# GpSimd's instructions of a decoder step issued in written order, with some mixer, feed-forward and tail steps in another order or on another engine

## The chip, the cores and the metric

The kernel runs on one core of one Trainium2 chip. The metric is the device time of one execution in microseconds (us): three runs of the kernel before took 1024.37, 1024.83 and 1026.25 us, so the median is 1024.83. The core's engines are TensorE (PE in the profile; PEld is its weight load), VectorE (DVE), ScalarE (ACT), GpSimd (POOL) and SyncE (SP), which here only issues transfers.

## The reference

One layer of a hybrid decoder is computed for 512 new prompt tokens behind 16 learned meta tokens, and for 8 running sequences of 4 new tokens each: 560 rows of 1024 in all. Cut to what matters:

```python
x = x + 0.5 * swiglu(rmsnorm(x, g_ff1), ...)          # FF1, 2816 hidden
u = rmsnorm(x, g_mix); z = u @ w_in                   # q, k, v, o, gates, x, y
# 4 mLSTM heads of 128: s = (q k^T) * exp(D - m); num = s v + w_inter * C0 q
#   den = sum(s) + w_inter * (n0 . q); h = num / max(|den|, exp(-m)); state C, n, m
# RG-LRU on 512 channels: causal conv of width 4, gates r and i,
#   h_t = a_t h_(t-1) + sqrt(1 - a_t^2) * i * xc
x = x + concat(mlstm, lru) @ w_out
x = x + 0.5 * swiglu(rmsnorm(x, g_ff2), ...)          # FF2
y = rmsnorm(x, g_final)                               # and all new states
```

## The kernel before, in words

The activations X stay in on-chip memory, transposed: 8 tiles of 128 channels by 560 rows. All products run in a split form: a number is taken apart into a high half that TensorE multiplies in one pass (whi, xh, made by a CAST on ScalarE, L259) and a low rest (wlo, xl, made on VectorE, L264), and three products replace one (L296). The weights come in tiles of 128x512 on SP's queue. The two feed-forward parts use a scheme with seven products of sums of blocks in place of eight (L409; sums on VectorE in L239 and L483). The mixer's first product begins at 384.8 us of the span, behind the first feed-forward part.

The order of the work is written out by hand: FF1, MID1, FF2, MID2 are lists of step names, and PLAN is that of the mixer. A step such as tk1 is do_tk(1); it issues a few instructions on several engines. For the engines in MANUAL (line 21) the instructions stay in the order in which the steps are written; before, these are TensorE, ScalarE and VectorE. GpSimd's instructions, and SP's, are put in an order of its own by a scheduler that reckons with modelled durations. Every engine executes its queue strictly in order, so an instruction that waits holds up all behind it on its engine.

The names that the change and the prediction's steps touch:

- acc (L378) sums the squares of X for the root of the norm, on GpSimd except the last; psn (L391) is its product with ones on TensorE.
- The mixer's set-up on GpSimd (L890 to L919): identity, masks, ones. do_wrg (L923 to L931, step rg) fills one of two gate matrices of the RG-LRU: a memset of wrg, two transfers into it, a CAST to wrgh, a subtraction to wrgl. rg1 is PLAN's first step.
- do_g (L960 to L975) is the gate product pgate. It takes two weight tiles, and for each copies 40 columns from wlo into whi on GpSimd (CAST whi<-wlo, L969), before TensorE's matmuls with that tile (L972).
- For a head h: evacuations k, q, v of the products to qT, kT, vT (L953, L955); tk and tv transpose kT and vT on TensorE (pt, L1297 to L1299), the last rows by way of a copy t on GpSimd (L1294); s and m make W, the weights times the score products (L1401, VectorE); sd adds W's pieces into D (L1407 to L1411, GpSimd); qw makes qw and qn (L1418, L1420, GpSimd); n is numerator and denominator (pn, L1430 to L1454, TensorE); cp scales the state c by its decay, eight instructions (L1512, GpSimd), and adds px (L1520, VectorE).
- For a channel tile: ex evacuates px into xp (L1112 to L1119; few columns on GpSimd, the rest on VectorE); cx is the convolution (L1127, L1129); cc makes a, th and its factors (L1175 to L1181, the last a memset of eight columns of a on GpSimd); cd multiplies them (L1187), copies eight columns into th on GpSimd (L1188), scans (L1190, VectorE) and copies the ends of hs into the output tile osm (L1191, L1192, GpSimd).
- The tail: st holds the products of three heads' final states, side by side in one bank (L815 to L818); state_out copies them out on ScalarE (L821, L822), and ScalarE's queue issues o_cp and o_small (L859, L860).

## Time and profile before

| | |
|---|---|
| median of three runs | 1024.83 us |
| the profiled execution's own time | 1024.98 us |
| its span (first to last instruction) | 1023.3 us |
| mean granted clock of TensorE | 0.995 |
| TensorE busy | 1010.1 us, 99% |
| VectorE busy | 831.6 us, 81% |
| ScalarE busy | 558.3 us, 55% |
| GpSimd busy | 119.8 us, 12% |
| transferred, mean rate | 102.85 MB, 101 GB/s |

The profile is of one execution. A timeline row gives start and length, the engine, the line, the operation, output<-inputs, shapes and a count of instructions that follow each other; in brackets stands how long the engine was idle before it, and what it waited for. The view of waits adds such idle times up by the line that waited and what released it. A window gives the busy time of each engine in a stretch, the clock that was granted to TensorE (1.00 is full speed), and the transfers.

### The profile page before, as it was taken

Reading aid. Unit: us, or ns where it says so; the run is one execution under the profiler, and the core shown is the slowest. Engines: PE = TensorE matmul, PEld = TensorE weight load, DVE = VectorE, ACT = ScalarE, POOL = GpSimd, SP = SyncE. Lnnn points to the kernel's source line nnn. Section 1 sums busy time; section 2 is a strip of 40 time slices with the busy share of each in tenths; the row PEclk is TensorE's granted clock in tenths of the full one; section 3 lists DMA queues with packets and bytes.
Section 4 is the critical chain, followed back from the end, with each engine's and each line's share of the span. In section 5 each row is a group of like instructions: output and inputs, shape, how many; then the busy total and the mean of one; then the engine's idle time right before and its main releaser. Section 6 shows DMA issues by size and latency. Waiting matters only on the chain.

```text
span 1023.3 us, 20215 instructions
## 1 busy us (share of the span) xinstructions
PE 1010.1 (99%) x7786; PEld 995.2 (97%) x7786; DVE 831.6 (81%) x1462; ACT 558.3 (55%) x1071; POOL 119.8 (12%) x198
## 2 busy tenths in 40 slices
PE   9999999999999999998999999999999999999998
PEld 8999999999999999998999999999999999999997
DVE  7988788888788797879888865799888899859774
ACT  6544555565544455475756743554555665654543
POOL 0000000000000035353651202100000000000002
PEclk9999999999999999998999999999999999999999
DMA  6222223223332334234142133223323323235222
GB/s 227 95 83 88 99 94 112 85 98 109 89 104 60 102 103 146 86 95 138 54 135 97 62 104 107 73 63 103 109 89 103 104 94 114 93 102 157 78 71 96
DMA packets 60985, 102.85 MB, mean 101 GB/s; under 512 B 8512, under 2 KB 16976, under 8 KB 60888
## 3 DMA queue, kind: packets, MB, share of 16 engines
q1 hardware_dynamic: 60200, 101.23, 30.8%
q8 instruction: 61, 1.00, 0.4%
q10 hardware_dynamic: 688, 0.32, 0.1%
q14 instruction: 36, 0.29, 0.1%
HBM read 95.20 MB, written 6.33 MB: 99 GB/s over the span
## 4 chain that ended last, share of the span: by engine, by line
PE 86%; DVE 7%; issue 2%; ACT 2%; POOL 2%; DMA 1%; SPq 0%; DVEq 0%; ACTq 0%; POOLq 0%
PE pb L409 27%; PE pad L409 20%; PE pd L296 15%; PE po L296 6%; PE pg L296 3%; PE pu L296 3%; PE pv L296 2%; PE py L296 2%; PE pq L296 2%; DVE wlo L264 2%; PE pd L792 1%; POOL c L1512 1%; PE px L296 1%; PE p L296 1%; PE pk L296 1%
## 5 line engine op out<-in xcount | busy, mean ns | idle before, releaser
L259 ACT CAST whi<-raw 128x512 fp32r<-128x512 f32 (+2 forms) x289 | 172.4, 606 | 160.7 <-PE pad L409 41.6
L264 DVE TENSOR_TENSOR wlo<-raw,whi 128x512 fp32r<-128x512 f32 (+2 forms) x289 | 197.2, 699 | 68.2 <-ACT whi L259 65.4
L259 ACT CAST whi<-s 128x512 fp32r<-128x512 f32 x180 | 111.8, 622 | 106.2 <-PE pb L409 36.4
L264 DVE TENSOR_TENSOR wlo<-s,whi 128x512 fp32r<-128x512 f32 x180 | 124.3, 692 | 12.6 <-ACT whi L259 6.5
L409 PE MATMUL pad<-q21h,whi 128*128 128x280 f32 (+1 forms) x360 | 104.2, 290 | 0.9 <-DVE X L483 0.9
L409 PE MATMUL pb<-qt4l,whi 128*128 128x280 f32 (+1 forms) x360 | 104.0, 289 | 0.0
L409 PE MATMUL pad<-q21l,whi 128*128 128x280 f32 (+1 forms) x360 | 104.0, 289 | 0.0
L409 PE MATMUL pad<-q21h,wlo 128*128 128x280 f32 (+1 forms) x360 | 104.0, 289 | 0.0
L409 PE MATMUL pb<-qt4h,whi 128*128 128x280 f32 (+1 forms) x360 | 103.9, 289 | 0.0
L409 PE MATMUL pb<-qt4h,wlo 128*128 128x280 f32 (+1 forms) x360 | 103.9, 289 | 0.0
L409 PEld LDWEIGHTS pad<-q21h,whi 128*128 128x128 f32 x360 | 67.8, 188 | 1.1 <-ACT whi L259 1.1
L409 PEld LDWEIGHTS pb<-qt4h,whi 128*128 128x128 f32 x360 | 67.9, 189 | 0.0
L409 PEld LDWEIGHTS pb<-qt4h,wlo 128*128 128x128 f32 x360 | 67.8, 188 | 0.0
L409 PEld LDWEIGHTS pb<-qt4l,whi 128*128 128x128 f32 x360 | 67.8, 188 | 0.0
L409 PEld LDWEIGHTS pad<-q21l,whi 128*128 128x128 f32 x360 | 67.8, 188 | 0.0
L409 PEld LDWEIGHTS pad<-q21h,wlo 128*128 128x128 f32 x360 | 67.8, 188 | 0.0
L239 DVE TENSOR_TENSOR s<-raw 128x512 f32<-128x512 f32 x90 | 61.5, 684 | 1.8 <-DMA raw<-in_wdn 1.8
L296 PE MATMUL pd<-hh,whi 128*128 128x280 f32 (+1 forms) x294 | 61.3, 290 | 0.6 <-ACT whi L259 0.4
L296 PE MATMUL pd<-hl,whi 128*128 128x280 f32 (+1 forms) x294 | 61.4, 290 | 0.2 <-DVE hl L557 0.2
L296 PE MATMUL pd<-hh,wlo 128*128 128x280 f32 (+1 forms) x294 | 61.2, 289 | 0.0
L378 POOL TENSOR_TENSOR acc<-acc,sq 128x560 f32<-128x560 f32 (+1 forms) x6 | 9.4, 1564 | 419.8 <-ACT sq L377 419.7
L409 PE MATMUL pb<-q11h,whi 128*128 128x280 f32 (+1 forms) x180 | 52.4, 291 | 0.0
(466 smaller groups left out, 2993.9 us busy)
## 6 DMA issues: line engine op xcount, KB each, us to landing
raw<-in_wgu SPq DMA_DIRECT2D x174, 256.0 KB, 2.7
raw<-in_wdn SPq DMA_DIRECT2D x71, 256.0 KB, 2.7
raw<-in_win SPq DMA_DIRECT2D x50, 256.0 KB, 3.3
raw<-in_wout SPq DMA_DIRECT2D x16, 256.0 KB, 3.1
raw<-in_wdn SPq DMA_DIRECT2D x18, 192.0 KB, 2.3
c<-in_c0t SPq DMA_DIRECT2D x4, 512.0 KB
out_o_cs<-c SPq DMA_DIRECT2D x4, 512.0 KB, 3.0
X<-in_xT SPq DMA_DIRECT2D x7, 280.0 KB, 5.0
```

Of the source, the lines that this page charges most:

```text
L239: dve.tensor_tensor(q[k], q[x], q[y], op=op)
L259: act.copy(ready[i][0][:, :src.shape[-1]], src)
L264: dve.tensor_tensor(lo, src, hi, op=ALU.subtract)
L296: state["mm"] = pe.matmul(ps[:, hf, :n], a[:, ws], b[k][:, c0 + hf * n:c0 + hf * n + n], start=first and j == 0 and i == 0, stop=last and ...
L378: (dve if d == KD - 1 else pool).tensor_tensor(self.acc[:, c0:], self.acc[:, c0:], s[:, c0:], op=ALU.add)
L409: pe.matmul(ps, a[:, k * P:k * P + P], b, start=first and k == 0 and i == 0, stop=k == KD // 2 - 1 and i == 2, skip_group_check=not first)
L792: pe.matmul(pd[d - TAIL][:, hf, :b - a], u[:, o:o + P], v[:, C16 + a:C16 + b], start=f == c0 and m == 0, stop=f == c1 - 1 and m == 2)
L1512: pool.tensor_scalar(c0[:, b, :], c0[:, b, :], Wb[:, b, 3:4], None, op0=ALU.mult)
```

## The change

1. GpSimd joins MANUAL: its instructions are issued in the order of the steps, like those of the other three engines.
2. In PLAN the steps gf, ge, L0, tv0, ek1, eq0 and ck1 change places; the eight scalings of c become a step of their own, cw, put behind n; cc of tile 1 is split: ci1 stands where cc1 stood, and cj1, which makes th, ti and the last form of a, behind cp0.
3. Few-column instructions of ex, cc, cd and tv (memsets and copies) go from GpSimd to VectorE. Wi's sum goes there too, and in exchange a minimum on E goes to GpSimd. The copies of m into om stand later.
4. qw adds W's last piece (32x32) into qn on GpSimd, so that n needs one matmul pair less (L1453 goes).
5. In FF1 the weight step w3 stands before the root; in MID1 ib3 and if3 before qe3; in FF2 the halves ei2, hi2, hj2 replace em2, hh2, hl2, and the residual steps rd change places.
6. In the tail each head's final state has its own bank, its copies and its transfer; y's tiles are shared out otherwise between GpSimd and VectorE; o_small goes out on SP's queue.

What GpSimd issues around the gate product, before. whi<-wlo are the gate's weights, wrg the RG-LRU's gate matrix; ones, ident and the masks are set-up:

```order
L378 TENSOR_TENSOR acc<-acc,z 128x560
L969 CAST whi<-wlo 128x4x40 x2
L378 TENSOR_TENSOR acc<-acc,sq 128x560
L890 MEMSET ident 128x128
...
L925 MEMSET wrg 128x512
L901 AFFINE_SELECT smask<-smask 32x32
L909 AFFINE_SELECT seqm<-seqm 32x8 x3
L929 CAST wrgh_5108<-wrg 128x512
L930 TENSOR_TENSOR wrgl_5109<-wrg,wrgh_5108 128x512
L925 MEMSET wrg 128x512
```

And in the changed kernel (its line numbers are 18 higher here):

```order
L378 TENSOR_TENSOR acc<-acc,z 128x560
L378 TENSOR_TENSOR acc<-acc,sq 128x560
L908 MEMSET ident 128x128
...
L943 MEMSET wrg 128x512
L919 AFFINE_SELECT smask<-smask 32x32
L927 AFFINE_SELECT seqm<-seqm 32x8 x3
L947 CAST wrgh_5108<-wrg 128x512
L948 TENSOR_TENSOR wrgl_5109<-wrg,wrgh_5108 128x512
L987 CAST whi<-wlo 128x4x40 x2
L943 MEMSET wrg 128x512
```

The two casts of the gate's weights have moved from ahead of the last acc addition to behind the set-up and the first gate matrix.

On GpSimd again, head 1's D, qw and qn, before; the copies of hs are those of channel tile 1, vT and kT those of the next transposes, c_5909 is head 1's state:

```order
L1409 TENSOR_TENSOR D<-D,W 128x272
L1418 TENSOR_TENSOR qw<-qT,Wb 128x32
L1410 TENSOR_TENSOR D<-D,W 128x144
L1420 TENSOR_TENSOR qn<-qw,C 128x32
L1411 TENSOR_TENSOR D<-D,W 16x16
L1294 COPY t_6663<-vT 128x96
L1294 COPY t_6778<-kT 128x96
L1512 TENSOR_SCALAR c_5909<-c_5909,Wb 128x128
L1188 COPY th<-C 128x8
L1512 TENSOR_SCALAR c_5909<-c_5909,Wb 128x128 x3
L1191 COPY osm<-hs 128x1
L1192 COPY osm<-hs 128x8
```

And in the changed kernel:

```order
L1438 TENSOR_TENSOR D<-D,W 128x272
L1439 TENSOR_TENSOR D<-D,W 128x144
L1440 TENSOR_TENSOR D<-D,W 16x16
L1220 COPY osm<-hs 128x1
L1221 COPY osm<-hs 128x8
L1447 TENSOR_TENSOR qw<-qT,Wb 128x32
L1449 TENSOR_TENSOR qn<-qw,C 128x32
L1451 TENSOR_TENSOR qn<-qn,W 32x32
L1540 TENSOR_SCALAR c_5909<-c_5909,Wb 128x128 x8
```

qw, which stood among the sums of D, now stands behind the two copies of hs, the scan's result; the sum with W is new; the eight scalings follow together, and the copy into th is VectorE's.

The diff, cut to its core:

```diff
-MANUAL = {mybir.EngineType.PE, mybir.EngineType.Activation, mybir.EngineType.DVE}
+MANUAL = {mybir.EngineType.Pool, mybir.EngineType.PE, mybir.EngineType.Activation, mybir.EngineType.DVE}
...
-x2 f0 cv1 p0 ex2 cf0 tk1 cp0 cx2 ck1
+x2 f0 cv1 p0 ex2 cf0 tk1 ck1 cp0 cj1 cx2
 q2 L2 s1 w1 m1 sd1 eq2 hx2 hq2
-v2 ev2 cd1 hd1 a2 ta2 ca2 b2 cb2 vm1 sk1 qw1 tb2 n1 cc2 cn1 hk2 ce0
+v2 ev2 cd1 hd1 a2 ta2 ca2 b2 cb2 vm1 sk1 qw1 tb2 n1 cw1 cc2 cn1 hk2 ce0
...
-y1 tk3 cf2 to1 hd3 ey1 gy1 ck3 so0 mo1 n3 sk3 cn3 cm3
+y1 tk3 cf2 to1 hd3 ey1 gy1 ck3 so0 mo1 n3 cw3 sk3 cn3 cm3
...
         def state(i):
-            py = st[:, 129 * i:129 * i + 129]
+            py = st[i] = mm_tile("st")[:, 0, :129]
...
         def state_out(i):
-            act.copy(cp[:, i, :], st[:, 129 * i:129 * i + P])
-            act.copy(osm[:, O_NP + i:O_NP + i + 1], st[:, 129 * i + P:129 * i + P + 1])
+            act.copy(cp[:, i, :], st[i][:, :P])
+            act.copy(osm[:, O_NP + i:O_NP + i + 1], st[i][:, P:])
+            nc.scalar.dma_start(o_cp[i], cp[:, i, :])
...
     def do_ex(ct):
-        pool.memset(xp[:, 0:3], 0.0)
-        pool.tensor_copy(smp(xp, 0, 3),
+        dve.memset(xp[:, 0:3], 0.0)
+        dve.tensor_copy(smp(xp, 0, 3),
...
     def do_cd(ct):
         dve.scalar_tensor_tensor(ti, ti, -1.0, tr, op0=ALU.mult, op1=ALU.mult)
-        pool.tensor_copy(ti[:, 528:584].rearrange("p (b j) -> p b j", j=7)[:, :, 2], C[:, H0 + 8 * ct:H0 + 8 * ct + 8])
+        dve.tensor_copy(ti[:, 528:584].rearrange("p (b j) -> p b j", j=7)[:, :, 2], C[:, H0 + 8 * ct:H0 + 8 * ct + 8])
...
     def do_qw(h):
         pool.tensor_tensor(qn, qw, n0.unsqueeze(2).to_broadcast([P, NB, 4]), op=ALU.mult)
+        qs = qn.rearrange("p b j -> p (b j)")[:32]
+        pool.tensor_tensor(qs, qs, d["W"][:32, WO[5]:WO[5] + 32], op=ALU.add)
...
     def do_n(h):
-        pe.matmul(pn[:, 1, 64:96], one_m[1][:32, :], W[:32, WO[5]:WO[5] + 32], start=True, stop=False)
-        pe.matmul(pn[:, 1, 64:96], one_m[1], d["qn"].rearrange("p b j -> p (b j)"), start=False, stop=True)
+        pe.matmul(pn[:, 1, 64:96], one_m[1], d["qn"].rearrange("p b j -> p (b j)"), start=True, stop=True)
...
+    def do_cw(h):
+        c0, Wb = D[h]["c0"], D[h]["Wb"]
+        for b in range(NB):
+            pool.tensor_scalar(c0[:, b, :], c0[:, b, :], Wb[:, b, 3:4], None, op0=ALU.mult)
...
     def do_cp(h):
-        for b in range(NB):
-            pool.tensor_scalar(c0[:, b, :], c0[:, b, :], Wb[:, b, 3:4], None, op0=ALU.mult)
```

## The prediction

> **What bounds the kernel now.** I read the page first, for the engines' shares. Its first lines:

> ```profile
> span 1023.3 us, 20215 instructions
> PE 1010.1 (99%) x7786; PEld 995.2 (97%) x7786; DVE 831.6 (81%) x1462; ACT 558.3 (55%) x1071; POOL 119.8 (12%) x198
> ```

> TensorE is busy for 1010.1 of 1023.3 us. So an edit counts by three things only: matmuls taken out, stalls of TensorE removed or made, and the clock at which it runs. GpSimd with its 12% has no throughput to speak of here; it counts by when it hands a tile over. Next the waits of TensorE, the longest first:

> ```profile
> PE pt L1297 <- DVE xp L1117: 4.0, 1, 4.0
> PE pad L409 <- DVE X L483: 0.9, 1, 0.9
> PE pd L296 <- ACT whi L259: 0.4, 1, 0.4
> PE pq L296 <- DVE kT L955: 0.3, 1, 0.3
> PE pd L296 <- DVE hl L557: 0.2, 1, 0.2
> PE pu L296 <- DVE wlo L264: 0.2, 1, 0.2
> ```

> One wait of 4.0 us is most of what there is to win. The timelines of TensorE, VectorE and GpSimd around it (start, length, engine; idle time before it in brackets) say how it came about:

> ```profile
> 460.76 0.21 POOL L1525 TENSOR_TENSOR osm<-C,Wb 128x8 f32<-128x8 f32 x1 [3.07 <-DMA Wb<-rows]
> 461.18 1.38 DVE L1190 TENSOR_TENSOR_SCAN hs<-a,th 128x584 f32<-128x584 f32 x1 [4.52 <-POOL th L1188]
> 468.57 0.17 PE L1502 MATMUL py<-wm,K5s 96*128 96x8 f32 x1
> 472.74 1.09 PE L1297 MATMUL pt<-ident,kT 128*128 128x128 f32 x4 [4.00 <-DVE xp L1117]
> ```

> GpSimd, in the scheduler's order, waits 3.07 us for a transfer, and only then copies the eight columns (L1188) for which VectorE's scan has been waiting 4.52 us. VectorE stays late from there on and frees the bank of px (L1117, its last read) just before 472.74, although px and the products behind it, up to py at 468.57, were long done. Then the windows (us, busy time of PE, PEld, DVE, ACT, POOL, granted clock, DMA) and TensorE's rows behind the wait:

> ```profile
> 470.00:472.00 2.00, 0.00 (x0) 0.00 (x0) 1.96 (x5) 0.00 (x0) 0.11 (x1) 0.63 0.06 11
> 476.77 0.65 PE L296 MATMUL pq<-xh,whi 128*128 128x272 f32 x2
> 477.22 0.48 PE L296 MATMUL pq<-xl,whi 128*128 128x272 f32 x2
> 478.80 0.42 PE L296 MATMUL pq<-xl,whi 128*128 128x272 f32 x2
> 479.06 0.41 PE L296 MATMUL pq<-xh,wlo 128*128 128x272 f32 x2
> ```

> The clock falls to half inside the stall (0.63 on the mean of 470 to 472 puts the fall at 470.5) and stays there until about 477.3, 4.6 us after TensorE goes on. In that time pairs of matmuls start 0.45 us apart (476.77 to 477.22) instead of 0.26 (478.80 to 479.06), so 4.6 x (1 - 0.26/0.45) = 2.0 us more is lost: the stall's whole price is 5.9 to 6.0 us.

> **What the change removes.** Three short waits have their late producer moved ahead in VectorE's order: X (L483) before a wlo at FF1's end, kT before the zl products, one wlo before FF1's root: 0.9 + 0.3 + 0.2 = -1.4 us. In FF2 the wait for hl (0.2) gets its product in halves, and the one for a weight (0.4) an earlier release; I take -0.4 (0 to -0.6), since another product may be late behind them. The four pairs of 32-column matmuls of the denominators go:

> ```profile
> 452.29 0.38 PE L1453 MATMUL pn<-W,ones 32*128 32x32 f32 x2
> 452.60 0.41 PE L1454 MATMUL pn<-qn,ones 128*128 128x32 f32 x2
> ```

> A pair holds TensorE for 452.60 - 452.29 = 0.31 us, four of them -1.2 us. For the 4.0 us stall: the eight-column copy is VectorE's own now, so nothing of GpSimd stands ahead of the scan, and VectorE's work behind the copy is no more than before. VectorE would have about 4.5 us in hand against 4.0 lost, and ex2 follows px at once. What is late next is the evacuation itself, about 0.2 us behind the end of py. So -3.9 and -2.0 for the clock: -5.9 us (0 if VectorE is late for another reason, which the windows below speak against).

> In the tail three pairs of copies and two DMA issues on ScalarE stand behind the last state product:

> ```profile
> 1019.02 0.27 ACT L821 COPY cp<-st 128x128 f32<-128x128 f32 x1 [3.85 <-PE st L818]
> 1019.60 0.22 ACT L822 COPY osm<-st 128x1 f32<-128x1 f32 x1
> 1020.27 0.49 ACTq L860 DMA_DIRECT2D out_o_small<-osm  x1
> ```

> With a bank for each state, two pairs (0.4 of the 0.6 us from 1019.02 to the last copy's start at 1019.60) go beside products, and the second issue (0.49) goes to another queue: -0.9 us; -0.2 if the y transfers, now shared out otherwise between queues, end last.

> **What it adds: the gate product.** This is the largest term. The timeline of GpSimd and TensorE at the stage's start:

> ```profile
> 382.64 0.98 POOL L969 CAST whi<-wlo 128x160 fp32r<-128x160 f32 x2 [2.23 <-DVE wlo L264]
> 384.47 1.68 POOL L378 TENSOR_TENSOR acc<-acc,sq 128x560 f32<-128x560 f32 x1 [0.84 <-ACT sq L377]
> 388.05 0.82 POOL L891 TENSOR_SCALAR_AFFINE_SELECT ident<-ident 128x128 f32<-128x128 f32 x1
> 388.83 0.28 POOL L895 TENSOR_SCALAR_AFFINE_SELECT cmask<-cmask 128x128 f32<-128x128 f32 x1
> 391.43 0.51 POOL L925 MEMSET wrg<- 128x512 f32 x1
> 395.25 0.67 POOL L929 CAST wrgh<-wrg 128x512 fp32r<-128x512 f32 x1 [2.35 <-DMA wrg<-in_wrg]
> 396.01 1.45 POOL L930 TENSOR_TENSOR wrgl<-wrg,wrgh 128x512 fp32r<-128x512 f32 x1
> 391.98 0.63 PE L972 MATMUL pgate<-xh,whi 128*128 128x280 f32 x2
> ```

> The scheduler had put the two casts that finish the gate's weights in front, long before TensorE wants them at 391.98. In written order they stand behind the mixer's set-up and behind rg1 (memset wrg, its DMAs, wrgh, wrgl), since rg1 is the first step of the plan. GpSimd's chain from the last acc add on: set-up and memset end 5.8 us after 386.15 (391.43 + 0.51), less 0.1 for the two V memsets that leave; then 3.3 us to the data; 0.76 to wrgl's start; 1.45; the first cast 0.7 (two span 0.98). Together 11.9 us, so the first gate matmul may start 386.15 + 11.9 = 398.05 by the old clock, where it started at 391.98: a wait of 6.1 us. What comes earlier in the feed-forward part moves both ends alike. TensorE executes in order, so px and all behind it wait too, and nothing covers it. The ends: 3.7, worked out with the first rival, and 6.4 with both casts needed. The stall is longer than the one of 4.0 us that halved the clock, so I add the same 2.0 (1.0 to 3.0, by where the next change of the clock falls): **+8.1 us**.

> By the rows above the clock fell some 1.8 us after TensorE's last matmul (470.5 against 468.57 + 0.17), and a stall of 4.0 us cost 2.0 us more. [...]

> **n1, head 1's denominators.** Rows of VectorE, GpSimd and TensorE, and of GpSimd in the next head:

> ```profile
> 490.32 0.74 DVE L953 TENSOR_TENSOR vT<-pv,r 128x560 f32<-128x560 f32 x1 [1.14 <-PE pv L296]
> 490.97 0.76 DVE L1187 SCALAR_TENSOR_TENSOR th<-th 128x584 f32<-128x584 f32 x1
> 492.88 1.53 DVE L1190 TENSOR_TENSOR_SCAN hs<-a,th 128x584 f32<-128x584 f32 x1 [1.15 <-POOL th L1188]
> 487.03 0.69 POOL L1418 TENSOR_TENSOR qw<-qT,Wb 128x32 f32<-128x32 f32 x1
> 491.71 0.50 PE L1430 MATMUL pn<-qw,c 128*128 128x4 f32 x4
> 522.10 0.19 POOL L1192 COPY osm<-hs 128x8 f32<-128x8 f32 x1
> 518.52 0.25 POOL L1418 TENSOR_TENSOR qw<-qT,Wb 128x32 f32<-128x32 f32 x1
> ```

> Before, GpSimd made qw at 487.03, 4 us ahead of need. Now the two copies of hs stand ahead of qw, so n1 waits for vT, th, scan, two copies, qw: vT and th end at 491.7, the columns' copy 0.1, scan 1.53, a hand-over 0.1, two copies and qw 0.6 by the light rows (0.19 a copy, 0.25 qw): 494.1 to 494.3, against 491.71. That is +2.6; with copies and qw at their slow rows (qw 0.69) about 3.6. VectorE itself has also more to do in this stretch: before, it reached vT with 1.14 us to spare, having started at 471.72; now it starts within 0.2 us of TensorE's transposes, and cj1's products (th, ti and a, some 2 us) come into the stretch, while TensorE gains the 2.0 us of the clock. That makes vT 0 to 1.7 us late; I take 1.2. So +3.8 (2.6 to 5.3). A stall of 3.8 us lies nearest to the one of 4.0 that halved the clock; I take +1.8 (0 to 2.0). Sum **+5.6 us**.

> **Heads 2 and 3.** GpSimd now adds W's last piece into qn ahead of D, and ahead of tk3's copy t:

> ```profile
> 564.01 0.21 POOL L1411 TENSOR_TENSOR D<-D,W 16x16 f32<-16x16 f32 x1
> 564.76 0.27 PE L1299 MATMUL pt<-ident,t 128*96 128x128 f32 x1
> ```

> D starts with the last piece of W instead of the first, which I put at 0.8 us later: its end 564.22 + 0.8, then the copy, 0.2 to 0.6 like the copies above, 565.2 to 565.6 against 564.76, with TensorE 0.3 ahead for the pair taken out: +1.0 (0.4 to 1.3). In head 2 all eight scalings stand ahead of tv3's copy: +0.3 (0 to 0.8). The 22 few-column instructions that VectorE takes over, 0.1 to 0.2 us each by the osm rows, are some 3 us over 200 us; I take 0, their cover being VectorE's idle time; without it, see the third rival. The window of the fullest part:

> ```profile
> 500.00:520.00 20.00, 20.00 (x156) 19.46 (x155) 19.02 (x31) 13.85 (x34) 5.98 (x16) 1.00 0.30 80
> ```

> **Sum.** -1.4 - 0.4 - 1.2 - 5.9 - 0.9 + 8.1 + 5.6 + 0.3 + 1.0 = +5.2 us. On the profiled execution's own 1024.98 us (its span of 1023.3 and 1.7 around it) that gives 1030.2; the median of the three runs, 1024.83, is 0.15 lower, so 1030.0 us.

> **Rivals.** First, the other side: GpSimd runs the set-up at its light pace. ident took 0.82 us and cmask, of one shape and operation, 0.28. There are five like ident (smask, two selects of seqm, wrgl); at about 0.5 each, an estimate from that pair, 2.4 us go, and the gate waits 3.7 without losing the clock; n1 at its light 2.6, also at full clock. The sum is -1.4 - 0.4 - 1.2 - 5.9 - 0.9 + 3.7 + 2.6 + 0.3 = -3.2, 1021.6 us. It turns where gate and n1 together cost under 13.7 - 5.2 = 8.5 us. Against it: VectorE does the same work beside the set-up as before. [...] Chance 0.08.

> Second, n1's stall stays small: VectorE carries a lead out of the gate's stall, n1 costs 2.6 with no loss of clock: 1027.0 us. Against it: px ties VectorE to TensorE again just before. Chance 0.16.

> Third, VectorE becomes the bound in the mixer: 19.02 of 20 us are busy in the fullest window, and the 3 us of small instructions, with 1 to 2 us of waits for each other, come out at the end: +4 to +5, 1034.5 us. It decides where VectorE has under 0.5 us in 20 to spare. Chance 0.12.

> Fourth, the change does not put the casts behind rg1 in effect: TensorE's wait turns out to be on an earlier count. Then 8.1 goes: 1021.9 us. The order of the instructions speaks against it. Chance 0.03.

> **How the numbers follow.** The forecast keeps 0.61. A measurement of this kernel can tell some 0.2% from no change, 2 us: 1022.8 to 1026.9. Faster: rivals one and four, 0.11. Same: half of the second rival (0.08) and the forecast with gate and n1 both at their lower ends (0.04), 0.12. Slower: the rest, 0.77. The range leaves out the first and fourth rival below (0.11) and the worst third of the third above (0.04): 1023.5 to 1035.0.

> **What would show it.** In the changed profile: a wait of about 6 us of pgate for the cast of whi, a window at half clock behind it; none at tk1; one of 3 to 4 us at pn for qw; no L1453 pair. I am wrong if pgate starts within 2 us of psn, or if pn follows the gates' products at once.

## The result, and the profile after

The changed kernel takes 1043.72 us (median of 6 runs, 1036.73 to 1044.99), the kernel before 1025.07 us (6 runs, 1024.37 to 1026.25): the ratio is 1.0171, with a 95% interval of 1.0144 to 1.0199. The change makes the kernel 18.7 us slower, where +5.2 us was forecast. The sign was right, the size 3.6 times too small, and the time lies outside the range. Runs of one kernel lie up to 9 us apart here, the longer ones at a lower mean clock (0.985 at 1039.57 us against 0.995 at 1030.56 in qw_ahead), so each median stands with its lowest and highest run.

The profiled execution took 1044.99 us. The head of its page:

```profile
span 1043.3 us, 20212 instructions
PE 1020.1 (98%) x7778; PEld 1004.0 (96%) x7778; DVE 835.2 (80%) x1484; ACT 559.1 (54%) x1072; POOL 122.9 (12%) x183
```

TensorE is busy for 10 us more with eight matmuls fewer. That alone says that half of the loss is no wait but slower matmuls. The other half stands in the waits of TensorE:

```profile
PE pn L1461 <- POOL qw L1447: 6.2, 1, 6.2
PE pgate L990 <- POOL whi L987: 5.6, 1, 5.6
PE pt L1328 <- POOL t L1323: 2.2, 1, 2.2
PE pv L296 <- DVE xl L367: 1.1, 1, 1.1
PE pden L1469 <- ACT zh L1293: 1.0, 1, 1.0
PE pl L1238 <- DVE c L1554: 0.8, 1, 0.8
```

The stall of 4.0 us at tk1 is gone, as are the short ones for X, kT, wlo and in FF2. In their place stand three waits for GpSimd, 14.0 us together, and three short ones. All idle time of TensorE up to its own last matmul comes to 19.0 us, against 8.9 before.

The first of the three is the gate product. GpSimd's timeline there:

```profile
382.21 1.63 POOL L378 TENSOR_TENSOR acc<-acc,sq 128x560 f32<-128x560 f32 x1 [2.99 <-ACT sq L377]
393.88 0.92 POOL L947 CAST wrgh<-wrg 128x512 fp32r<-128x512 f32 x1 [2.93 <-DMA wrg<-in_wrg]
394.89 1.41 POOL L948 TENSOR_TENSOR wrgl<-wrg,wrgh 128x512 fp32r<-128x512 f32 x1
396.25 0.80 POOL L987 CAST whi<-wlo 128x160 fp32r<-128x160 f32 x2
```

The casts of the gate's weights come last of this row of work, as forecast, 14 us after the acc addition began. The second is at tv0, in GpSimd's timeline and then TensorE's:

```profile
428.82 1.61 POOL L1054 TENSOR_SCALAR E<-E 4x560 f32<-4x560 f32 x1 [6.01 <-ACT E L1052]
430.67 0.26 POOL L1323 COPY t<-vT 128x96 f32<-128x96 f32 x1
430.98 0.32 PE L1328 MATMUL pt<-ident,t 128*96 128x128 f32 x1 [2.15 <-POOL t L1323]
```

The copy t, whose vT was there since the start of the mixer, stands behind the minimum on E, which the change gave to GpSimd and which waits 6.01 us for ScalarE. The third is n1. VectorE, GpSimd and TensorE:

```profile
496.38 0.73 DVE L971 TENSOR_TENSOR vT<-pv,r 128x560 f32<-128x560 f32 x1
498.02 1.38 DVE L1219 TENSOR_TENSOR_SCAN hs<-a,th 128x584 f32<-128x584 f32 x1
499.46 0.57 POOL L1220 COPY osm<-hs 128x1 f32<-128x1 f32 x1 [3.56 <-DVE hs L1219]
499.96 1.20 POOL L1221 COPY osm<-hs 128x8 f32<-128x8 f32 x1
501.13 0.70 POOL L1447 TENSOR_TENSOR qw<-qT,Wb 128x32 f32<-128x32 f32 x1
501.88 1.01 PE L1461 MATMUL pn<-qw,c 128*128 128x4 f32 x4 [6.20 <-POOL qw L1447]
512.71 0.81 PE L296 MATMUL px<-xh,whi 128*128 128x280 f32 x2
514.26 0.67 PE L296 MATMUL px<-xh,whi 128*128 128x280 f32 x2
514.72 0.67 PE L296 MATMUL px<-xl,whi 128*128 128x280 f32 x2
```

GpSimd has nothing to do for 3.56 us, with qw's operands long there, since the copies of hs ahead of it wait for the scan. When qw has come, n1 needs 10.8 us, from 501.88 to 512.71. In the kernel before it began at 491.71, and px followed it after 5.9 us:

```profile
497.61 0.50 PE L296 MATMUL px<-xh,whi 128*128 128x280 f32 x2
```

The windows of the changed kernel (busy time of PE, PEld, DVE, ACT, POOL, then the granted clock) say why:

```profile
396.00:400.00 4.00, 3.17 (x13) 3.17 (x14) 1.34 (x2) 0.00 (x0) 1.51 (x4) 0.50 0.14 32
432.00:436.00 4.00, 4.00 (x21) 3.74 (x21) 3.57 (x9) 1.73 (x6) 1.95 (x4) 0.62 0.23 76
504.00:508.00 4.00, 4.00 (x12) 2.80 (x12) 2.17 (x5) 0.00 (x0) 4.00 (x5) 0.50 0.00 0
508.00:512.00 4.00, 4.00 (x14) 2.70 (x12) 0.00 (x0) 0.00 (x0) 1.77 (x4) 0.50 0.00 0
516.00:520.00 4.00, 4.00 (x25) 4.00 (x24) 1.75 (x3) 2.16 (x4) 0.00 (x0) 0.72 0.37 131
```

In the stall at n1 the clock fell to half, and although TensorE then shows as busy without a gap, it stayed there through all of n1 and 5.5 us of px, until about 518.2. The changes of the clock lie at 395.4 (for 6.8 us), 432.9 (3.4), 497.8 (20.5) and 589.9 (3.4): 34 us at half clock up to the last product, against 6.8 before.

### The profile page after: what moved, and what is told of

Its sections match the earlier page's. It is cut to its first block, busy times and chain, and to the rows that moved or that the text cites. A ratio compares the mean times of both kernels' runs of the same rounds, so it can differ in the third digit from the quotient of the medians.

```text
span 1043.3 us, 20212 instructions
## 1 busy us (share of the span) xinstructions
PE 1020.1 (98%) x7778; PEld 1004.0 (96%) x7778; DVE 835.2 (80%) x1484; ACT 559.1 (54%) x1072; POOL 122.9 (12%) x183
## 4 chain that ended last, share of the span: by engine, by line
PE 87%; DVE 5%; ACT 2%; POOL 2%; issue 2%; DMA 1%; SPq 0%; DVEq 0%; POOLq 0%; ACTq 0%
PE pb L409 26%; PE pad L409 20%; PE pd L296 15%; PE po L296 6%; PE pu L296 4%; PE pg L296 4%; PE px L296 3%; PE pk L296 2%; PE pq L296 1%; PE py L296 1%; DVE wlo L264 1%; PE pn L1465 1%; PE pd L808 1%; PE pgate L990 1%; PE p L296 1%
## 5 line engine op out<-in xcount | busy, mean ns | idle before, releaser
L259 ACT CAST whi<-raw 128x512 fp32r<-128x512 f32 (+2 forms) x289 | 172.8, 606 | 179.9 <-PE pad L409 41.3
L264 DVE TENSOR_TENSOR wlo<-raw,whi 128x512 fp32r<-128x512 f32 (+2 forms) x289 | 197.6, 700 | 71.2 <-ACT whi L259 68.6
L259 ACT CAST whi<-s 128x512 fp32r<-128x512 f32 x180 | 111.7, 622 | 105.1 <-PE pb L409 36.5
L264 DVE TENSOR_TENSOR wlo<-s,whi 128x512 fp32r<-128x512 f32 x180 | 124.2, 691 | 12.9 <-ACT whi L259 6.5
L409 PE MATMUL pad<-q21h,whi 128*128 128x280 f32 (+1 forms) x360 | 104.2, 290 | 0.2 <-DVE z L428 0.2
L409 PE MATMUL pb<-qt4l,whi 128*128 128x280 f32 (+1 forms) x360 | 104.0, 289 | 0.0
L409 PE MATMUL pad<-q21l,whi 128*128 128x280 f32 (+1 forms) x360 | 104.0, 289 | 0.0
L409 PE MATMUL pad<-q21h,wlo 128*128 128x280 f32 (+1 forms) x360 | 104.0, 289 | 0.0
L409 PE MATMUL pb<-qt4h,whi 128*128 128x280 f32 (+1 forms) x360 | 103.9, 289 | 0.0
L409 PE MATMUL pb<-qt4h,wlo 128*128 128x280 f32 (+1 forms) x360 | 103.9, 289 | 0.0
L409 PEld LDWEIGHTS pad<-q21h,whi 128*128 128x128 f32 x360 | 67.8, 188 | 0.4 <-DVE z L428 0.4
L409 PEld LDWEIGHTS pb<-qt4h,whi 128*128 128x128 f32 x360 | 67.9, 189 | 0.0
L409 PEld LDWEIGHTS pb<-qt4h,wlo 128*128 128x128 f32 x360 | 67.8, 188 | 0.0
L409 PEld LDWEIGHTS pad<-q21l,whi 128*128 128x128 f32 x360 | 67.8, 188 | 0.0
L409 PEld LDWEIGHTS pb<-qt4l,whi 128*128 128x128 f32 x360 | 67.8, 188 | 0.0
L409 PEld LDWEIGHTS pad<-q21h,wlo 128*128 128x128 f32 x360 | 67.8, 188 | 0.0
L296 PE MATMUL pd<-hl,whi 128*128 128x280 f32 (+1 forms) x294 | 61.6, 290 | 0.0
L296 PE MATMUL pd<-hh,whi 128*128 128x280 f32 (+1 forms) x294 | 61.4, 290 | 0.0
L296 PE MATMUL pd<-hh,wlo 128*128 128x280 f32 (+1 forms) x294 | 61.2, 289 | 0.0
L378 POOL TENSOR_TENSOR acc<-acc,sq 128x560 f32<-128x560 f32 (+1 forms) x6 | 9.3, 1543 | 423.1 <-ACT sq L377 423.0
L409 PE MATMUL pb<-q11h,whi 128*128 128x280 f32 (+1 forms) x180 | 52.4, 291 | 0.0
```

What stands on the lines that cost most here:

```text
L259: act.copy(ready[i][0][:, :src.shape[-1]], src)
L264: dve.tensor_tensor(lo, src, hi, op=ALU.subtract)
L296: state["mm"] = pe.matmul(ps[:, hf, :n], a[:, ws], b[k][:, c0 + hf * n:c0 + hf * n + n], start=first and j == 0 and i == 0, stop=last and ...
L378: (dve if d == KD - 1 else pool).tensor_tensor(self.acc[:, c0:], self.acc[:, c0:], s[:, c0:], op=ALU.add)
L409: pe.matmul(ps, a[:, k * P:k * P + P], b, start=first and k == 0 and i == 0, stop=k == KD // 2 - 1 and i == 2, skip_group_check=not first)
```

## The experiments

Theory A: GpSimd's written order puts three hand-overs behind work for which nobody waits; each stall costs its length and a stretch at half clock, and at n1 that stretch is long since n's own matmuls do not bring the clock back. Rival B: VectorE, with 22 instructions more and cj1's products in another place, sets the mixer's pace. Rival C: the clock is a state of the run, and no consequence of the stalls. Each ratio is to the kernel before on the same chip (medians of 1024.6 to 1025.0).

**gate_ahead.** Only the gate's place on GpSimd:

```diff
-rg1
-v0 gn gs0 gs1 g gr0 gr1 ev0 rg0
+v0 gn gs0 gs1 g rg1 gr0 gr1 ev0 rg0
```

> The changed kernel with step rg1 put behind g, so that GpSimd casts the gate's weights right after the set-up, ahead of the memset, the transfers and the split of the first gate matrix. Theory A (GpSimd's written order puts a hand-over behind work that nobody waits for; each stall of TensorE costs its length and a stretch at half clock): the wait of 5.6 us at pgate goes to under 0.5 us, the half-clock stretch of 6.8 us behind it goes, and the time falls by 5.6 + 2.3 = 7.9 us, from 1043.7 to about 1035.8 us. Rival B (VectorE, with its 22 added instructions, is what sets the mixer's pace): what is won at the gate is lost again at the next wait of TensorE for VectorE, and the time stays within 2 us of 1043.7.

It took 1037.54 us (6 runs, 1029.71 to 1037.85), 6.2 less than the changed kernel, where 7.9 were expected. The wait at pgate went altogether, and with it the stretch at half clock at 395 (mean clock 0.987, in the changed kernel 0.982). A little was given back at tv0, where TensorE now arrives sooner:

```profile
PE pt L1327 <- POOL t L1322: 3.0, 1, 3.0
```

A holds, with 0.8 us of the gain moved to the next late hand-over.

**qw_ahead.** Only n1:

```diff
-v2 ev2 cd1 hd1 a2 ta2 ca2 b2 cb2 vm1 sk1 qw1 tb2 n1 ...
+v2 ev2 qw1 cd1 hd1 a2 ta2 ca2 b2 cb2 vm1 sk1 tb2 n1 ...
```

> The changed kernel with qw1 put ahead of cd1, so that GpSimd makes qw before the two copies of hs for which it waits for VectorE's scan. Theory A: the wait of 6.2 us at n1 goes (0 to 1 us is left), the clock stays full, n1 takes 5.6 us instead of 10.8 and the px behind it 2.5 us less: 6.2 + 5.2 + 2.5 = 13.9 us less, about 1030 us. Rival B: VectorE's lateness is the cause, n1 then waits for VectorE's zl or ScalarE's zh instead, 4 us or more, the clock still drops, and at most 3 us are won: 1041 us or more.

It took 1035.10 us (4 runs, 1030.56 to 1039.57). The waits:

```profile
PE pgate L990 <- POOL whi L987: 5.0, 1, 5.0
PE pn L1461 <- POOL qn L1451: 1.6, 1, 1.6
```

The place behind hs was worth 4.6 of 6.2 us. But the profiled run was still at half clock for 10.2 us from 497.5 on (mean clock 0.988): 1.6 us of idle time ahead of n1 were enough here. Between A and B on the size; the wait itself is A's.

**n1_filled and n1_filled_long.** The stall at n1 is filled with products of channel tile 2 that are computed again into their own bank and change nothing (bb2 is b2's product three times, or seven times in the long version); qw comes no sooner:

```diff
-... a2 ta2 ca2 b2 cb2 vm1 sk1 qw1 tb2 n1 ...
+... a2 ta2 ca2 b2 bb2 cb2 vm1 sk1 qw1 tb2 n1 ...
```

> The changed kernel with the second gate product of channel tile 2 repeated three more times into its own bank (36 matmuls, the same values): 4.8 us of work that is thrown away, in the stall at n1. qw comes when it came before, so n1 starts no earlier. Theory A (the clock falls in the stall, and n's own matmuls do not bring it back, so that 20.5 us run at half clock): the clock stays full through n1, n1 takes 5.6 us instead of 10.8, px 2.5 us less: 7.7 us less for 4.8 us more work, about 1036 us. Rival C (n1 is slow for its operands or its waits, not for the clock; or the clock is a state of the run): the time is 1043.7 us or more, and n1 still takes 10 us.

The expectation counts a product as 12 matmuls; it has 6, so the filling was 18 matmuls and 2.4 us. The time was 1043.90 us, unchanged:

```profile
501.53 1.01 PE L1471 MATMUL pn<-qw,c 128*128 128x4 f32 x4 [3.79 <-POOL qw L1457]
```

The 3.8 us that were left idle still halved the clock (n1 took 10.8 us, 501.53 to 512.36, and px's pairs start 0.47 us apart), so the run decided nothing. With seven repetitions:

> The changed kernel with the second gate product of channel tile 2 repeated seven times (42 matmuls, thrown away): 5.6 us of work in n1's stall of 6.2, where the shorter filling left 3.8 us idle and the clock still fell. Theory A: under 1 us of idle time is left, the clock stays full through n1 and px: 5.2 + 2.5 = 7.7 us less than the changed kernel, 1036 us, with n1 at 5.6 us. Rival C (n1 takes its 10.8 us for its operands or waits, or the clock is a state of the run): 1043.7 us.

It took 1036.29 us (4 runs, 1034.64 to 1039.94), 7.4 us less than the changed kernel, for 5.6 us of thrown-away work. TensorE's timeline and a window:

```profile
501.40 0.61 PE L1471 MATMUL pn<-qw,c 128*128 128x4 f32 x4 [0.57 <-POOL qw L1457]
507.18 0.50 PE L296 MATMUL px<-xh,whi 128*128 128x280 f32 x2
```

```profile
504.00:508.00 4.00, 4.00 (x27) 3.28 (x26) 1.62 (x4) 0.62 (x3) 4.00 (x5) 1.00 0.00 0
```

n1 starts as late as in the changed kernel (501.40 and 501.88), and takes 5.8 us instead of 10.8, at a clock of 1.00. That settles the clock: the stall caused it, C falls, and its price at n1 is 7 to 8 us.

**three_ahead.** gate_ahead and qw_ahead together, and tv0's copy t issued ahead of gd, so ahead of the sums R and the minimum on E.

> The changed kernel with three of GpSimd's hand-overs put ahead: rg1 behind g, qw1 ahead of cd1, and tv0's copy t of vT ahead of the sums R and of the minimum on E. Theory A: the waits of 5.6, 6.2 and 2.2 us and the clock's 2.3, 7.7 and 1.5 us behind them go: 25.5 us less, 1018 us, 7 us under the kernel before. Rival B: VectorE's pace shows instead, and the time stays above 1030 us.

It took 1021.45 us (10 runs, 1018.74 to 1026.62), ratio to the kernel before 0.9977 (0.9954 to 0.9999): the three hand-overs account for the whole loss, though the median is 3.5 us above the 1018 expected. n1 still waits 1.6 us, and in the profiled run the clock stayed full there (px's pairs start 0.26 us apart); it fell for 6.8 us at n3 (mean clock 0.994).

**written_only.** The kernel before with GpSimd in MANUAL, and nothing else (one line).

> The kernel before with one line changed: GpSimd joins MANUAL, nothing else. Theory A: the gate waits 5 to 6 us and loses 2.3 us to the clock, n1 waits 4 to 6 us behind the copies of hs and loses 5 to 8 us to the clock; the stall at tk1 goes with its clock (-5.9), since the scalings of c stand behind tk1 in written order: 1024.6 + 7.9 + 12 - 5.9 = 1038 to 1040 us. Rival B: without the 22 instructions on VectorE and without cj1's move the written order alone costs nothing at n1: 1028 us or less.

It took 1053.84 us (ratio 1.0284, 1.0267 to 1.0301):

```profile
PE pt L1299 <- POOL t L1294: 5.4, 1, 5.4
PE pl L1209 <- DVE c L1520: 5.1, 1, 5.1
PE pgate L972 <- POOL whi L969: 5.1, 1, 5.1
PE pn L1430 <- POOL qw L1418: 4.6, 1, 4.6
```

The written order alone costs more than the whole change, and 14 us more than the 1038 to 1040 expected. Two more stalls of 5 us appear: at head 1's transposes, where t stands behind eight-column work that waits for VectorE, and at pl. So the change's other parts, the few-column steps on VectorE and cw among them, take back 10 us of what its first line costs. Rival B falls as the cause of the loss: VectorE has none of its new work here.

**pool_scheduled.** The reverse: all of the change but the line on MANUAL.

> The changed kernel with one line undone: GpSimd is taken out of MANUAL again, so the scheduler orders it, and all else of the change stays (steps in another order, few-column steps on VectorE, cw, the tail). Theory A: the three hand-overs come early again (the order shows the casts of the gate's weights ahead of the set-up, t<-vT ahead of R, qw ahead of hs), so the waits of 5.6, 2.2 and 6.2 us and 11.5 us of the clock's cost go; what remains are the gains, 1.4 + 0.8 + 1.2 + 5.9 us: about 1016 us. Rival B (VectorE, with its 22 added instructions and cj1's later place, sets the pace): 1030 us or more.

It took 1022.62 us (9 runs, 1018.46 to 1024.88), ratio 0.9972 (0.9954 to 0.9990). The waits for GpSimd are gone, but n1 waits for VectorE, and the clock then fell for 13.7 us (mean clock 0.992):

```profile
PE pn L1461 <- DVE vT L971: 1.9, 1, 1.9
PE pv L296 <- DVE xl L367: 1.5, 1, 1.5
```

So B has a part: behind GpSimd's lateness stood VectorE's.

**pool_scheduled_cc and pool_scheduled_hq.** Two ways to make VectorE reach vT sooner, both with the scheduler's order on GpSimd; the first two lines are _cc, the last two _hq:

```diff
-k2 ca1 cb1 ek2 ci1 tv1 am1
-x2 f0 cv1 p0 ex2 cf0 tk1 ck1 cp0 cj1 cx2
+k2 ca1 cb1 ek2 cc1 tv1 am1
+x2 f0 cv1 p0 ex2 cf0 tk1 ck1 cp0 cx2
...
-q2 L2 s1 w1 m1 sd1 eq2 hx2 hq2
-v2 ev2 cd1 hd1 ...
+q2 L2 s1 w1 m1 sd1 eq2 hx2
+v2 ev2 hq2 cd1 hd1 ...
```

> The changed kernel with GpSimd left to the scheduler and, besides, cc1 whole in its old place (cj1's products of about 2 us on VectorE are taken back out of the stretch between px's evacuation and vT). Theory D (what is left at n1 is VectorE's lateness with vT, 1.9 us of stall and 13.7 us at half clock in the profiled run, and cj1's later place makes it): n1 does not wait, the clock stays full there, and tk1 waits about 1 us for xp instead, as in the run with only the eight columns on VectorE; all runs lie near 1018.5 us instead of between 1018.5 and 1024.9. Rival E (vT's lateness comes from other work): n1 still waits 1 to 2 us, and runs near 1024 remain.

> The changed kernel with GpSimd left to the scheduler, cj1 as changed, and hq2 (1.2 us of VectorE's zl for head 2, needed one head later) put behind ev2, so that vT comes 1.2 us earlier. Theory D: n1's wait falls from 1.9 to about 0.7 us, too short to halve the clock; runs near 1017 us, few or none above 1020. Rival E: as before, between 1018.5 and 1024.9 us.

_cc took 1018.42 us (4 runs, 1017.97 to 1019.20), ratio 0.9937 (0.9922 to 0.9952), the fastest of all; _hq took 1019.73 us (1018.85 to 1020.81), ratio 0.9949 (0.9935 to 0.9964). Neither waits at n1; the waits of _cc:

```profile
PE pv L296 <- DVE xl L367: 1.5, 1, 1.5
PE pt L1326 <- DVE xp L1136: 1.4, 1, 1.4
```

With cc1 whole, 1.4 us come back at tk1, but the clock stays full there (mean clock 1.000). With hq2 behind, 1.4 us come up at the product of head 1's norm (pv waits for sqh). D holds for the wait: either move removes it, the clock stays full in both (mean clock 1.000 and 0.999), and of the two only cj1's place is the change's doing. On the time, _hq lies 2.7 us above the 1017 expected.

**ahead_all.** Written order, with all late hand-overs put ahead at once (rg1, tu0, qw1, the sum with W as a step behind D, hq2, hd3).

> The changed kernel in written order throughout, with every late hand-over put ahead: rg1 behind g, tv0's copy t ahead of R, qw1 ahead of s1 with the sum with W as a step of its own behind D, the same split in the other heads, hq2 behind ev2, hd3 ahead of cf2. Theory A with D: no stall over 1.5 us is left, the clock stays full from 10 us on: 1018.7 (the best runs with three hand-overs ahead) less up to 1.5 us at n1 and 0.7 at n3, 1016.5 to 1018 us in all runs, 0.7% under the kernel before. Rival: other stalls come up in their place, 1020 us or more.

It took 1021.22 us (10 runs, 1020.73 to 1026.22), ratio 0.9967 (0.9956 to 0.9978). n1 does not wait and nine of ten runs are within 1.4 us, but the rival is right on the size. The waits below are n3's and that of the product of head 1's norm, where the clock fell for 3.4 us (mean clock 0.997):

```profile
PE pn L1470 <- DVE dd L1529: 1.2, 1, 1.2
PE pv L1522 <- ACT sqh L1512: 1.2, 1, 1.2
```

**th_vector.** The kernel before with one part of the change, the eight-column memset and copy on VectorE:

```diff
-        pool.memset(a0[:, 528:584]...
+        dve.memset(a0[:, 528:584]...
...
-        pool.tensor_copy(ti[:, 528:584]...
+        dve.tensor_copy(ti[:, 528:584]...
```

> The kernel before with one part of the change: the memset of eight columns of a and the copy of eight columns into th go from GpSimd to VectorE; GpSimd stays with the scheduler. Theory A: the scan no longer stands behind GpSimd's wait for Wb, tk1's wait of 4.0 us and its 2.0 us at half clock go, 1018.7 us. The rival (VectorE is late at tk1 for its own amount of work): under 1 us is won, 1024 us.

It took 1021.19 us (5 runs, all within 1 us), ratio 0.9965 (0.9952 to 0.9978), at a clock of 0.999:

```profile
PE pl L1209 <- DVE c L1520: 1.2, 1, 1.2
PE pt L1297 <- DVE xp L1117: 1.1, 1, 1.1
```

The cause of tk1's stall is as the prediction has it; 1.1 us of it remain, as VectorE's own work, and pl waits 0.9 us longer.

## Why the prediction was wrong, point by point

- **Gate product, +8.1.** Right: 5.6 us of wait, and 2.4 for the clock (5.4 us of matmuls at 0.47 us a pair instead of 0.26). gate_ahead took both away.
- **tk1, -5.9.** Right in mechanism and size in the whole change; th_vector shows that 1.1 us of it needs cj1's later place.
- **n1, +5.6: the step that failed.** The order was right (qw behind hs), and the wait was 6.2 us instead of 3.8, above the bound of 5.3. Before, vT began 1.4 us ahead of n1; with TensorE through at 495.68, 494.3 would have been in time, and it began at 496.38, 2.1 us late instead of 1.2. And copies and qw took their slow durations (0.57, 1.20 and 0.70 us), not the light ones that I chose, so that n1 came 5.5 us behind vT instead of 4.0. The greater error is the clock's term, 1.8 with a bound of 2.0. It was taken over from tk1, where a dense product follows the stall. Here n1 follows: its 5.6 us (5.9 before, less the pair taken out) became 10.8, and 5.5 us of px ran at 0.47 us a pair: 5.2 + 2.5 = 7.7 us. Together 13.9 instead of 5.6.
- **A row misread at n1.** The qw at 487.03 belongs to head 2, whose qT VectorE had just written (485.05), and so do qw and qn in the piece of the order under "The change"; the sums of D around them are head 1's. Head 1's qw stood much earlier, in the kernel before:

```profile
437.28 0.25 POOL L1418 TENSOR_TENSOR qw<-qT,Wb 128x32 f32<-128x32 f32 x1 [1.97 <-DVE qT L953]
```

The lead that the written order gave up was 54 us, not 4. The wait, reckoned from the hand-overs behind the scan, does not hang on that.
- **The first rival's sum.** It leaves out the 1.0 us of tk3 without a reason; with it the rival stands at 1022.6 us. Nothing hangs on that. Its full clock through stalls of 3.7 and 2.6 us was an assumption; no run shows it, and a stall of 3.79 us (n1_filled) and one of 2.15 (tv0) halved the clock.
- **tv0, not in the sum: +3.7.** 2.2 us of wait and 1.5 of clock. The prediction did not name the minimum on E among the steps that go to GpSimd, and so not what is queued behind its wait for ScalarE.
- **Heads 2 and 3, +1.3.** Nothing at tk3 and tv3, which do not wait. n3 costs 2.5 us for a cause that the prediction does not have: its pden waits 1.0 us for zh, and a stretch of 3.4 us at half clock follows (1.5 us). D is not late; its last sum ends 3.9 us before zh begins. ScalarE is: it loads the table for rs behind its wait for VectorE's dd, and before it loaded it ahead of that wait. The kernel before, then the changed one:

```profile
561.79 1.28 ACT L1491 ACT_TABLE_LOAD   x1
564.24 0.66 ACT L1491 ACTIVATE rs<-dd 128x544 f32<-128x544 f32 x1 [1.17 <-DVE dd L1490]
582.11 0.21 POOL L1440 TENSOR_TENSOR D<-D,W 16x16 f32<-16x16 f32 x1
582.39 1.28 ACT L1521 ACT_TABLE_LOAD   x1 [2.50 <-DVE dd L1520]
586.21 0.60 ACT L1293 CAST zh<-D 128x512 fp32r<-128x512 f32 x1
```

The load stands behind the wait in written_only too, and ahead of it in pool_scheduled, so it goes with the line on MANUAL; by what way is open.
- **FF1's waits, -1.4.** They went, and 1.1 came back as the wait of pv for xl, the next late thing, which the prediction asked for at tk1 and in FF2, but not here.
- **FF2, -0.4.** Three waits of 0.8 us went, one of 0.2 came.
- **The four pairs, -1.2.** The step of 0.31 us did not go with the pair: the next matmul now pays it; by what cause no run shows.

```profile
550.56 0.39 PE L1465 MATMUL pn<-W,V 16*128 16x16 f32 x2
550.88 0.41 PE L1484 MATMUL pn<-qn,ones 128*128 128x32 f32 x2
```

From pn's last narrow piece to the product with ones it is again 0.32 us; the whole of n2 is 0.23 us shorter (527.79 to 533.70 before, 545.45 to 551.13 after). So -0.9.
- **The tail, -0.9.** Nothing: 4.24 us from TensorE's end to the span's, 4.28 before. o_small moved to SP's queue, and there it waits behind the tiles of y:

```profile
1033.26 6.82 SPq L800 DMA_DIRECT2D out_y<-X  x5
1040.17 0.47 SPq L878 DMA_DIRECT2D out_o_small<-osm  x1
```

- **pl, not in the sum: +0.6** (0.8 us against 0.3).

The measured pieces add up: -0.3 for FF1, -0.6, -0.9, -6.0 at tk1, 0 in the tail, +8.0, +13.9, +3.7, +2.5 and +0.6 make +20.9, and the span grew by 20.0 us. Of the prediction's misses, n1's clock (5.9), n1's wait (2.4) and tv0 (3.7) make 12.0 of the 14.8 us by which the span's growth exceeds the sum.

What stays open: the measured pieces are those of one execution of 1044.99 us, the only one of the changed kernel with a trace. Another took 1036.73 us at a mean clock of 0.993 instead of 0.982. The distance fits n1's stretch at half clock, and the traces of qw_ahead and three_ahead show that one and the same stall there can bring it or not; that it was absent in that run is argued, not shown.

## What to carry to other kernels

An engine that is busy 12% of the time can cost 2.8% of the kernel by its order alone (written_only): in a queue that runs in the order of issue, as GpSimd's did here (3.56 us idle ahead of the copies of hs, with qw's operands long there), list for every hand-over what stands ahead of it, and for each of those what it waits for, tiny instructions above all. Price a stall of TensorE by what follows it: here the clock cost 2.0 us behind the 4.0 of tk1 and 2.4 behind the 5.6 of the gate, where dense matmuls follow, and 7.7 behind the 6.2 of n1, whose matmuls are narrow or unsplit. When a stall cannot be shortened, dense matmuls moved into it, even useless ones, may pay for themselves (n1_filled_long: 7.4 us won for 5.6 us of them); useful ones from behind it should be better, which no run tried.
